# Two more groups of the second down block by seven products, their sums of weights formed in HBM by adding transfers

## The chip, the cores and the metric

The kernel runs on one core of a Trainium2 chip. The metric is the device time of one execution in microseconds, a median over several runs. Engines are named as in the profile: PE (TensorE matmuls), PEld (its weight loads), DVE (VectorE), ACT (ScalarE), POOL (GpSimd), SP (SyncE, which here only issues transfers). Transfers run on 16 DMA engines, which the queues of SP, ACT and POOL share.

## What is computed

One layer on 256 tokens of width 2048, in float32: three kinds of attention, a gated merge, an output product, and a feed-forward part. The change is in the last product, `w_down`:

```python
h2 = rms_norm(x, g_ffn[l])
u = causal_depthwise_conv(h2 @ w_up[l], conv_w[l], conv_b[l])
u_gate, u_val = jnp.split(u, 2, axis=-1)
x = x + (jax.nn.silu(u_gate) * u_val) @ w_down[l]      # [256, 5632] @ [5632, 2048]
```

## The kernel before

**Precision.** Every weight tile is split into two float32r tiles, `hi` (a cast on ACT) and `lo = raw - hi` (a subtract on DVE). The activations are split in the same way. A product is three matmuls: `hi*hi`, `lo*hi`, `hi*lo` (`three`). Weights come from HBM through a ring of raw tiles (six of 128x1024 in the last stages), and `hi` and `lo` have four buffers each.

**The order of the stages.** The products of `mem` (`kv`, at the very start, one k of 128 rows at a time: 512 KB of `w_mem_kv`, and pieces of `mem`, then of `x`, which PE transposes), the projections with the attention heads between them, the gates, the branches and the merge, the output product, the up product with its convolution (from about 778 to 1232 us, a `tick` of the background work at every pair of k), and the down product in two blocks of 1024 columns (block 0 from about 1232 us, block 1 from 1344 us).

**Groups by eight or by seven.** A group of the down product is two k-tiles of 128 rows (`a_pair(p)`) by 1024 columns, and 256 tokens: a 2x2 by 2x2 block product with blocks of 128x128 and 128x512. `eight` does the eight block products, from two raw tiles. `seven` does seven, from sums of blocks of weights (T1, T2, T3, T4) and sums of blocks of activations (FS1 to FS4). The activation sums are made by `form` (and `pair_sums`), up to eight short operations on DVE and some casts on ACT. The weight sums are made ahead of time: `pair_sums_ahead` loads 1 MB of weights into SBUF, adds on DVE (`sums_in`), and stores the four sums to HBM in a tile `kept` (columns T1, T3, T4, T2 of `[P, 4, 512]`), mostly as background work in the up stage. `seven` then reads two of the blocks of `w_down` and the four sums: one whole raw tile (B10, B11), one of B00 and T3, one of T1 and T2, and half a tile of T4 (`junk`, two buffers).

**The plans.** A string says for each of a block's 22 groups whether it goes by eight (`e`) or by seven (`s`); `f` is a call of `form`, which readies the sums of the next pair. The sums of pairs 11 and later are kept where activations of pairs already used by an `e` lay (`s_of`). Block 0 has 11 sevens and 11 eights; block 1 has 14 and 8.

**What sets the order.** A scheduler places instructions on each engine as early as their inputs allow, unless they are pinned (`in_order`, `pin`). SP's queue takes loads in the order in which they were placed; each load waits until its raw tile is free, that is for the `lo` subtract of the tile six loads before. POOL has some masks to make at the start, transfers of small rows at 182 to 189 us and at 759 to 769 us, masks of attention heads between, and nothing else.

Of the kernel before, what the change touches and what calls it, by code (L numbers as in the profile page):

```python
# [13 lines left out]
ALU = mybir.AluOpType  # L14
# [19 lines left out]
PIECE = 1024  # L34
# [9 lines left out]
def hybrid_block(  # L44
# [25 lines left out]
    nc = tc.nc  # L70
# [31 lines left out]
    background = []  # L102
# [101 lines left out]
    def k_tiles(name):  # L204
# [23 lines left out]
    g_plans = (("", "esesesee", "esesesee"), ("esesesee", "esesesee", "esesesee"))  # L228
    d_plans = (
        "efefefef" + "sef" * 4 + "ssefsfssfssee",  # L230
        "efefef" + "sss" + "esss" * 3 + "ssee",
    )
    T1, T3, T4, T2 = range(4)
    FS2, FS4, FS3, FS1 = range(4)
    in_order = tc.keep_in_program_order
    dram = ctx.enter_context(tc.tile_pool(name="dram", bufs=1, space=bass.MemoryType.DRAM))
    by_k = lambda w: w[0].rearrange("(k p) n -> p k n", p=P)
# [6 lines left out]
        for name, w, plans in (("o", w_out, o_plans), ("d", w_down, d_plans))  # L244
        for nb, plan in enumerate(plans)
        for pr in pairs(name, plan.count("s"))
        for h in range(2)
    )

    def sums_in(w):  # L250
        both = w[:, 1:2].to_broadcast([P, 2, w.shape[2]])
        in_order(nc.vector.tensor_tensor(w[:, 0:2], w[:, 0:4:3], both, ALU.add))
        in_order(nc.vector.tensor_tensor(w[:, T2], w[:, T1], w[:, T2], ALU.add))
        in_order(nc.vector.tensor_tensor(w[:, T4], w[:, T2], w[:, T4], ALU.add))

    def kept_for(name, nb, pr):
        if (name, nb, pr) not in sums_of:
            at = f"kept_{name}{nb}_{pr}"
            sums_of[name, nb, pr] = dram.tile([P, 4, 512], F32, tag=at, name=at)
        return sums_of[name, nb, pr]  # L260
# [24 lines left out]
    def pair_sums_ahead(staging, period, add, store, most=99, delay=0):  # L285

        due = deque()
        clock = 0
        for _ in range(delay):
            yield  # L290

        def step():
            while due and due[0][0] <= clock:
                _, kept, w = due.popleft()
                in_order(nc.sync.dma_start(kept, w))

        periods = cycle(period if isinstance(period, tuple) else (period,))
        while len(halves) > 1 and halves[0][-1] == 0 and most:
            most -= 1
            name, wv, nb, pr, _ = halves.popleft()  # L300
            halves.popleft()
            kept = kept_for(name, nb, pr)
            w = staging(f"pre_{name}{nb}_{pr}")
            in_order(
                nc.sync.dma_start(
                    w.rearrange("p (k c) -> p k c", k=2), wv[:, 2 * pr : 2 * pr + 2, nb * PIECE : (nb + 1) * PIECE]
                )
            )
            w = w.rearrange("p (i c) -> p i c", i=4)
            due.append((clock + store, kept, w))  # L310
            for t in range(next(periods)):
                if t == add:
                    sums_in(w)
                step()
                clock += 1
                yield
        while due:
            step()
            clock += 1
            yield  # L320

    def first_sums():

        name, wv, nb, pr, _ = halves.popleft()
        halves.popleft()
        kept = kept_for(name, nb, pr)
        two = []
        for h in range(2):
            w = block(f"pre_{name}{nb}_{pr}_{h}").rearrange("p (i c) -> p i c", i=4)
            two.append(w)  # L330
            n0 = nb * PIECE + h * 256
            for n in range(2):
                in_order(
                    nc.sync.dma_start(
                        w.rearrange("p (k n) c -> p k n c", k=2)[:, :, n],
                        wv[:, 2 * pr : 2 * pr + 2, n0 + n * 512 : n0 + n * 512 + 256],
                    )
                )
            yield
            yield  # L340
        for w in two:
            sums_in(w)
            yield
        for _ in range(3):
            yield
        for h, w in enumerate(two):
            in_order(nc.sync.dma_start(kept[:, :, h * 256 : (h + 1) * 256], w))
            yield
# [475 lines left out]
    def in_turn(name):  # L824
        turn[0] += 1
        return staged[:, turn[0] % 2]

    background.append(pair_sums_ahead(in_turn, PF, 3, 7, most=14))
    qm = heads_of(block("qm"))
    y = norm_heads(ps, rstd, "mq")  # L830
# [348 lines left out]
    for nb, plan in enumerate(o_plans):  # L1179
# [19 lines left out]
    ends_tile = lambda name, dt: ff.tile([P, 2, PIECE], dt, tag="ends", bufs=1, name=name)  # L1199
    background.append(  # L1200
        pair_sums_ahead(lambda name: ends_tile(name, F32).rearrange("p i c -> p (i c)"), 8, 1, 5, delay=DU)
    )

    def a_pair(p):
        if p < FA // 2:
            return aT[:, 2 * p : 2 * p + 2]
        if not ends:
            ends.append(ends_tile("a_ends", F32R).rearrange("p i (k c) -> p i k c", k=2))
        return ends[0][:, p - FA // 2]
# [64 lines left out]
    for f0 in range(0, FT, 4):  # L1274
# [5 lines left out]
        for s in range(2):  # L1280
            ps = [bank(f"u{f0 + i}_{s}") for i in range(4)]
            c0 = s * D_FF + f0 * P
            for k in range(0, KT, 2):
                hi, lo = piece(upv[:, k : k + 2, c0 : c0 + 512], 2, 512, f"u{f0}_{s}_{k}")
                for j in range(2):
                    first, last = k + j == 0, k + j == KT - 1
                    for i in range(4):
                        c = slice(i * P, (i + 1) * P)
# [23 lines left out]
    N0, N1 = (plan.count("s") for plan in d_plans)  # L1312
# [3 lines left out]
    a_blocks = aT.rearrange("p k (l t q) -> p k l t q", l=2, t=NT)  # L1316
    formed = [0]

    def s_of(p, f):


        if f == FS1:
            return a_blocks[:, 2 * p, :, 1]
        if p < 9:
            return sf[:, 3 * p + f]
        if p == 9:
            return sf_more[0][:, f] if f < 2 else sf_rest[2]
        if p == 10:
            return sf[:, 27] if f == 0 else sf_rest[f - 1]
        return a_blocks[:, 2 * (p - N0 + N1) + f // 2, :, f % 2]  # L1330

    tmp_d = lambda name: place([P, PIECE], F32, "ts", name)

    def form():
        p = formed[0]
        formed[0] += 1
        if p == 9:
            sf_rest.extend(cst.tile([P, 2, P], F32R, tag=tag, name=f"sf_{tag}") for tag in ("rbc", "taps", "rows"))
        if p < 9:
            groups = [(sf[:, 3 * p : 3 * p + 3], slice(0, 3))]  # L1340
        elif p == 9:
            sf_more.append(place([P, 2, 2, P], F32R, "sf", "sf_more"))
            groups = [(sf_more[0], slice(0, 2)), (sf_rest[2], 2)]
        else:
            groups = [(s_of(p, f), f) for f in range(3)]
        pair_sums(a_pair(p), tmp_d(f"fw_{p}"), groups + [(s_of(p, FS1), FS1)])
# [4 lines left out]
    for nb, plan in enumerate(d_plans):  # L1351
        apart = [] if nb == 1 else None
        X = blocked(
            "d", w_down, nb, nb * PIECE, plan, lambda p, j: a_pair(p)[:, j], s_of, raw_d, junk,
            lambda n0, Y: gather(n0, Y, tmp_d), None, form, apart,
        )
        for t in range(NT):
            for n in range(2):
                c = nb * PIECE + n * 512
                o = xres[:, t, c : c + 512]  # L1360
                nc.vector.tensor_tensor(o, o, X[t][n], ALU.add)
                if (nb, t, n) == (1, 1, 1):
                    nc.scalar.dma_start(ov[:, t, c : c + 256], o[:, :256])
                    c, o = c + 256, o[:, 256:]
                    nc.vector.tensor_tensor(o, o, apart[0], ALU.add)
                    nc.scalar.dma_start(ov[:, t, c : c + 256], o)
                else:
                    nc.scalar.dma_start(ov[:, t, c : c + 512], o)
# [31 lines left out]
```

## Time and profile before

| | us |
|---|---|
| median of 3 runs | 1460.6 (1460.43, 1460.6, 1470.62) |
| the profiled execution | 1459.85 |
| its span, first to last instruction | 1458.1 |
| PE busy, by the records | 1452.6 |
| DVE busy | 1222.1 |
| ACT busy | 852.3 |
| DMA, mean of the span | 266 GB/s |

Times in the profile are counted from the start of the span. Busy time of PE counts matmuls whose ends are modelled and which overlap, so the distance from one matmul's start to the next says more than the length of one. A wait is idle time of an engine put down to what ended it.

### The profile page before, as it was taken

To read this page: it belongs to the slowest core of one execution; us is meant where nothing else is said; L and a number is where in the kernel's file an instruction comes from. 1 tells how busy PE (TensorE), PEld (TensorE's weight loads), DVE (VectorE), ACT (ScalarE), POOL (GpSimd) and SP (SyncE) were. 2 spreads that over 40 slices of the span, in tenths; PEclk is the share of its full clock that TensorE was granted. 3 is DMA by queue.
4 is the path that set the end of the run, shared out by engine and by line. 5 is a ranking of instruction groups with operands and counts; after the bars stand their busy time and mean duration, and the time that the engine had idled before them with its cause. 6 is when DMAs were issued, how large, how long until landed. Compare 5 with 4: busy or idle time off the path is not lost.

```text
span 1458.1 us, 20568 instructions
## 1 busy us (share of the span) xinstructions
PE 1452.6 (100%) x7295; PEld 1228.6 (84%) x7295; DVE 1222.1 (84%) x1804; ACT 852.3 (58%) x1210; POOL 21.4 (1%) x52
## 2 busy tenths in 40 slices
PE   9999999999999999999999999999999999999998
PEld 7888888888888888888888888888888888888887
DVE  5788778776898899998987888888888877999878
ACT  6755445464564556546766656556556565676665
POOL 0000010010000000000000000000000000000000
PEclk9999999999999999999999999999999999999999
DMA  8797999777668576788877888888888866789896
GB/s 294 227 351 246 324 330 329 261 256 218 205 210 267 174 227 200 269 269 263 300 214 233 290 273 299 283 269 300 287 278 299 271 197 201 255 282 339 297 333 218
DMA packets 166502, 387.64 MB, mean 266 GB/s; under 512 B 12554, under 2 KB 29854, under 8 KB 162174
## 3 DMA queue, kind: packets, MB, share of 16 engines
q1 hardware_dynamic: 164702, 383.29, 79.7%
q10 hardware_dynamic: 1328, 2.11, 0.4%
q8 instruction: 57, 0.93, 0.3%
q0 software_dynamic: 368, 0.93, 0.2%
q14 instruction: 47, 0.39, 0.1%
HBM read 347.47 MB, written 38.80 MB: 265 GB/s over the span
## 4 chain that ended last, share of the span: by engine, by line
PE 94%; DVE 3%; issue 2%; DMA 1%; POOL 0%; ACT 0%; DVEq 0%; POOLq 0%; ACTq 0%
PE u L1289 22%; PE u L1290 11%; PE xd L362 4%; PE xd L360 4%; PE xd L361 3%; PE xg L362 3%; PE xg L360 3%; PE xg L361 3%; PE s L362 2%; PE f L362 2%; PE s L360 2%; PE f L360 2%; PE f L361 2%; PE b L362 2%; PE s L361 2%; PE b L360 2%
## 5 line engine op out<-in xcount | busy, mean ns | idle before, releaser
L1289 PE MATMUL u<-hT,hi_u 128*128 128x512 f32 x1232 | 428.3, 394 | 0.0
L1290 PE MATMUL u<-hT,lo_u 128*128 128x256 f32 x1232 | 341.3, 277 | 0.0
L144 DVE TENSOR_TENSOR lo_u<-raw_u,hi_u 128x1024 fp32r<-128x1024 f32 x176 | 215.0, 1222 | 73.3 <-ACT hi_u L143 72.5
L1289 PEld LDWEIGHTS u<-hT,hi_u 128*128 128x128 f32 x1232 | 231.0, 188 | 53.6
L143 ACT CAST hi_u<-raw_u 128x1024 fp32r<-128x1024 f32 x176 | 184.7, 1050 | 133.8 <-PE u L1289 99.4
L1290 PEld LDWEIGHTS u<-hT,lo_u 128*128 128x128 f32 x1232 | 231.3, 188 | 0.0
L355 DVE TENSOR_TENSOR lo_d<-raw_d,hi_d 128x1024 fp32r<-128x1024 f32 x88 | 106.8, 1222 | 16.5 <-ACT hi_d L354 14.1
L354 ACT CAST hi_d<-raw_d 128x1024 fp32r<-128x1024 f32 x88 | 91.8, 1054 | 39.3 <-PE xd L361 13.1
L354 ACT CAST hi_g<-raw_g 128x1024 fp32r<-128x1024 f32 (+1 forms) x80 | 77.1, 972 | 49.4 <-PE xg L361 19.4
L355 DVE TENSOR_TENSOR lo_g<-raw_g,hi_g 128x1024 fp32r<-128x1024 f32 (+1 forms) x80 | 88.6, 1119 | 4.1 <-ACT hi_g L354 4.1
L361 PE MATMUL xg<-hi_g,xT 128*128 128x512 f32 x175 | 68.1, 389 | 0.0
L362 PE MATMUL xg<-lo_g,xT 128*128 128x512 f32 x175 | 68.1, 389 | 0.0
L360 PE MATMUL xg<-hi_g,xT 128*128 128x512 f32 x175 | 68.1, 389 | 0.0
L143 ACT CAST hi_f<-raw_f 128x1024 fp32r<-128x1024 f32 (+1 forms) x40 | 38.5, 967 | 46.3 <-PE f L361 29.4
L144 DVE TENSOR_TENSOR lo_s<-raw_s,hi_s 128x1024 fp32r<-128x1024 f32 (+1 forms) x40 | 44.5, 1119 | 23.8 <-ACT hi_s L143 23.8
L1289 PE MATMUL u<-hT_rest,hi_u 128*128 128x512 f32 x176 | 62.0, 394 | 0.0
L143 ACT CAST hi_b<-raw_b 128x1024 fp32r<-128x1024 f32 x32 | 33.7, 1053 | 45.9 <-PE b L361 20.3
L143 ACT CAST hi_s<-raw_s 128x1024 fp32r<-128x1024 f32 (+1 forms) x40 | 38.4, 962 | 37.7 <-PE s L361 26.8
L1240 ACT ACTIVATE y<-u,taps 128x256 f32<-128x256 f32 x88 | 49.6, 596 | 16.8 <-DVE u L1235 16.7
L144 DVE TENSOR_TENSOR lo_f<-raw_f,hi_f 128x1024 fp32r<-128x1024 f32 (+1 forms) x40 | 44.4, 1116 | 17.4 <-ACT hi_f L143 17.2
L362 PE MATMUL xd<-lo_d,aT 128*128 128x512 f32 x148 | 57.6, 389 | 0.0
L360 PE MATMUL xd<-hi_d,aT 128*128 128x512 f32 x148 | 57.6, 389 | 0.0
(551 smaller groups left out, 3482.0 us busy)
## 6 DMA issues: line engine op xcount, KB each, us to landing
raw_u<-in_w_up_dram SPq DMA_DIRECT2D x176, 512.0 KB, 4.8
raw_g<-in_w_in_dram SPq DMA_DIRECT2D x96, 512.0 KB, 4.5
raw_d<-in_w_down_dram SPq DMA_DIRECT2D x63, 512.0 KB, 5.5
pre_d<-in_w_down_dram SPq DMA_DIRECT2D x17, 1024.0 KB, 7.4
kept_d<-pre_d SPq DMA_DIRECT2D x17, 1024.0 KB, 7.0
raw_f<-in_w_in_dram SPq DMA_DIRECT2D x32, 512.0 KB, 5.6
raw_s<-in_w_in_dram SPq DMA_DIRECT2D x32, 512.0 KB, 6.1
raw_t_d<-kept_d SPq DMA_DIRECT2D x25, 512.0 KB, 5.8
```

The lines of the kernel that those rows point to most:

```text
L143: pin(nc.scalar.copy(hi[:, :m], raw[:, :m]))
L144: pin(nc.vector.tensor_tensor(lo[:, :m], raw[:, :m], hi[:, :m].bitcast(F32), ALU.subtract))
L354: nc.scalar.copy(hi[:, :n], src)
L355: nc.vector.tensor_tensor(lo[:, :n], src, hi[:, :n].bitcast(F32), ALU.subtract)
L360: fix(nc.tensor.matmul(o, lhsT=ah, rhs=w[0], start=first, stop=False))
L361: fix(nc.tensor.matmul(o, lhsT=al, rhs=w[0], start=False, stop=False))
L362: fix(nc.tensor.matmul(o, lhsT=ah, rhs=w[1], start=False, stop=last))
L1240: nc.scalar.activation(y, u[:, 2:], AF.Identity, scale=tap(2), bias=tap(3))
L1289: nc.tensor.matmul(ps[i], lhsT=hi[:, j, c], rhs=hT(k + j), start=first, stop=False)
L1290: nc.tensor.matmul(ps[i][:, :S], lhsT=lo[:, j, c], rhs=hT(k + j)[:, :S], start=False, stop=last)
```

## The change

Block 1 of the down product gets 16 sevens and 6 eights. The plan has two more `s` and `f` and is laid out anew; the activation sums of pairs 11 to 15 lie three to a pair, densely, behind the 32 k-tiles that belong to sevens (`s_of`). The weight sums of pairs 14 and 15 of this block (`in_hbm`) don't go through SBUF and DVE: a new generator, `sums_in_hbm`, issues five transfers for each on POOL's queue. The first copies the four blocks of weights from `w_down` into `kept`, the next four add one block onto another in place: T1 = B00 + B01, T3 = B01 + B11, T2 = T1 + B11, T4 = T2 + B10.

```diff
     d_plans = (
         "efefefef" + "sef" * 4 + "ssefsfssfssee",
-        "efefef" + "sss" + "esss" * 3 + "ssee",
+        "efsss" * 3 + "efssfsssssee",
     )
+    in_hbm = (("d", 1, 14), ("d", 1, 15))
...
         for pr in pairs(name, plan.count("s"))
+        if (name, nb, pr) not in in_hbm
         for h in range(2)
...
+    def sums_in_hbm(delay, period):
+        for _ in range(delay):
+            yield
+        for name, nb, pr in in_hbm:
+            kept = kept_for(name, nb, pr)
+            wv = by_k(w_down)[:, 2 * pr : 2 * pr + 2, nb * PIECE : (nb + 1) * PIECE]
+            b = wv.rearrange("p k (n c) -> p k n c", n=2)
+            nc.gpsimd.dma_start(kept.rearrange("p (k n) c -> p k n c", k=2), b)
+            for _ in range(period):
+                yield
+            for dst, src in ((0, b[:, 0, 1]), (1, b[:, 1, 1]), (3, kept[:, 0]), (2, kept[:, 3])):
+                nc.gpsimd.dma_start(kept[:, dst], src, accum_op=ALU.add)
+                for _ in range(period):
+                    yield
...
+    background.append(sums_in_hbm(40, 8))
...
-        return a_blocks[:, 2 * (p - N0 + N1) + f // 2, :, f % 2]
+        i = 3 * (p - N0) + f
+        return a_blocks[:, 2 * N1 + i // 2, :, i % 2]
```

The generator waits for 40 ticks of the up stage before its first transfer, but these transfers aren't pinned. POOL's order, before, from its last masks at the start of the kernel to the first mask of an attention head (`kept_d_14` and `kept_d_15` are the sums of pairs 14 and 15, `ck_row` and `ck` the small rows at 182 to 189 us):

```order
L557 AFFINE_SELECT upto<-ones_r 128x128
L561 AFFINE_SELECT after_r<-ones_r 128x128
L897 DMA ck_row_1832<-logits 128x2x4
L897 DMA ck_row_1836<-logits 128x2x2
L899 DMA ck_1834<-ck_row_1832 128x1024
L899 DMA ck_1838<-ck_row_1836 128x512
L926 AFFINE_SELECT fx_1959<-fx_1959 128x128 x2
```

And the same place now:

```order
L578 AFFINE_SELECT after_r<-ones_r 128x128
L331 DMA kept_d_14_7922<-in_w_down_dram 256x1x1024
L331 DMA kept_d_15_9059<-in_w_down_dram 256x1x1024
L335 DMA kept_d_14_7922<-in_w_down_dram 128x512 x2
L335 DMA kept_d_15_9059<-in_w_down_dram 128x512 x2
L335 DMA kept_d_14_7922<-kept_d_14_7922 128x512
L335 DMA kept_d_15_9059<-kept_d_15_9059 128x512
L335 DMA kept_d_14_7922<-kept_d_14_7922 128x512
L335 DMA kept_d_15_9059<-kept_d_15_9059 128x512
L914 DMA ck_row_1832<-logits 128x2x4
```

All ten transfers stand at the start of POOL's program, ahead of everything that POOL does for the attention; the only waits among them are those of each add for the transfers of its own pair.

DVE at the seam of the two down blocks, before (`xres_again` is the residual, to which block 0's last bank `xd_1_1` is added; `fw` and `aT` are the steps of `form`; `lo_d_30` is the split of k-tile 30, `lo_t_d_0` that of the sums of pair 0):

```order
L1361 TENSOR_TENSOR xres_again<-xres_again,xd_1_1_11735 128x512
L369 TENSOR_TENSOR fw_12858<-aT 128x512
L355 TENSOR_TENSOR lo_d_30_12874<-raw_d_30_12871,hi_d_30_12873 128x1024
L372 TENSOR_TENSOR fw_12858<-fw_12858 128x256
L373 SCALAR_TENSOR_TENSOR fw_12858<-fw_12858 128x128
L355 TENSOR_TENSOR lo_d_31_12892<-raw_d_31_12889,hi_d_31_12891 128x1024
L374 TENSOR_TENSOR fw_12858<-fw_12858 128x128
L378 TENSOR_TENSOR aT<-fw_12858,aT 128x128 x4
L355 TENSOR_TENSOR lo_d_32_12923<-raw_d_32_12920,hi_d_32_12922 128x1024
L369 TENSOR_TENSOR fw_12907<-aT 128x512
L355 TENSOR_TENSOR lo_d_33_12941<-raw_d_33_12938,hi_d_33_12940 128x1024
```

And now:

```order
L1380 TENSOR_TENSOR xres_again<-xres_again,xd_1_1_11746 128x512
L386 TENSOR_TENSOR fw_12870<-aT 128x512
L372 TENSOR_TENSOR lo_d_0_12897<-raw_d_0_12887,hi_d_0_12896 128x1024
L389 TENSOR_TENSOR fw_12870<-fw_12870 128x256
L390 SCALAR_TENSOR_TENSOR fw_12870<-fw_12870 128x128
L372 TENSOR_TENSOR lo_d_1_12907<-raw_d_1_12890,hi_d_1_12906 128x1024
L391 TENSOR_TENSOR fw_12870<-fw_12870 128x128
L395 TENSOR_TENSOR aT<-fw_12870,aT 128x128 x4
L372 TENSOR_TENSOR lo_t_d_0_12917<-raw_t_d_0_12892,hi_t_d_0_12916 128x1024
L372 TENSOR_TENSOR lo_t_d_0_12927<-raw_t_d_0_12894,hi_t_d_0_12926 128x512
L386 TENSOR_TENSOR fw_13061<-aT 128x512
L372 TENSOR_TENSOR lo_d_2_12943<-raw_d_2_12933,hi_d_2_12942 128x1024
```

The first seven of block 1 (pair 0) follows its first eight (pair 16) at once, where two more eights stood between; the second `form` stands behind the splits of that seven.

## The prediction

> **What bounds the kernel now.** I read the page first: busy times, then the slices.
>
> ```profile
> PE 1452.6 (100%) x7295; PEld 1228.6 (84%) x7295; DVE 1222.1 (84%) x1804; ACT 852.3 (58%) x1210; POOL 21.4 (1%) x52
> PE   9999999999999999999999999999999999999998
> PEclk9999999999999999999999999999999999999999
> DMA  8797999777668576788877888888888866789896
> ```
>
> TensorE is busy in every slice at its full clock, while the DMA engines are 60 to 90% busy. Matmul ends are modelled, so I went next to the waits of PE over the whole span; these two rows are all there are.
>
> ```profile
> PE spare L93 <- DVE qscale L565: 1.2, 1, 1.2
> PE s L362 <- DVE lo_s L144: 0.2, 1, 0.2
> ```
>
> Nothing holds PE up after the first 1.2 us. The span is its matmuls laid end to end; the timeline gives their pitch, here at the start of down block 1 (rows 3 matmuls apart).
>
> ```profile
> 1343.81 0.39 PE L360 MATMUL xd<-hi_d,aT 128*128 128x512 f32 x1
> ...
> 1344.49 0.39 PE L360 MATMUL xd<-hi_d,aT 128*128 128x512 f32 x1
> ...
> 1345.85 0.39 PE L360 MATMUL xd<-hi_d,aT 128*128 128x512 f32 x1
> ```
>
> Nine matmuls take 2.04 us: 0.227 us each, not the 0.39 of one record. So two things decide: how many matmuls go, and whether any supply of PE becomes late. A microsecond lost anywhere is lost for good, since PE has no later wait to make it up in.
>
> **Part 1, the products.** `eight` calls `three` 8 times (24 matmuls), `seven` 7 times (21). Two groups change from one to the other: 6 x 0.227 = 1.4 us less on PE. This lies on the path: **-1.4**.
>
> **Part 2, the supply of down block 1.** A seven needs 3.5 splits of 1024 columns where an eight needs 2, so DVE gets 2 x 1.5 = 3 more subtracts; and `form` runs 5 times there, not 3.
>
> ```profile
> L355 DVE TENSOR_TENSOR lo_d<-raw_d,hi_d x45: 1214/1224/1226, 1334.9 to 1445.4; 128x1024 fp32r<-128x1024 f32 x45
> L369 DVE TENSOR_TENSOR fw<-aT x3: 682/684/693, 1344.8 to 1355.3; 128x512 f32<-128x512 f32 x3
> L372 DVE TENSOR_TENSOR fw<-fw x3: 415/415/417, 1346.5 to 1357.1; 128x256 f32<-128x256 f32 x3
> L378 DVE TENSOR_TENSOR aT<-fw,aT x12: 280/284/286, 1348.5 to 1360.3; 128x128 fp32r<-128x128 f32 x12
> 1340.00:1350.00 10.00, 10.00 (x46) 8.29 (x45) 9.93 (x18) 4.78 (x8) 0.00 (x0) 1.00 0.96 319
> 1350.00:1360.00 10.00, 10.00 (x46) 8.29 (x45) 9.34 (x19) 5.19 (x12) 0.00 (x0) 1.00 0.89 305
> 1420.00:1430.00 10.00, 10.00 (x46) 8.25 (x45) 8.11 (x8) 7.37 (x8) 0.00 (x0) 1.00 0.92 328
> ```
>
> (In the window rows: length, then PE, PEld, DVE, ACT and POOL busy, granted clock, DMA share, GB/s.) Three subtracts are 3.7 us; a form is 0.68 + 0.42 + two 128-column steps at about 0.28 + 4 x 0.28 = 2.8, two are 5.6. DVE gets 9.3 us more over some 100 us. It is 99 and 93% busy only where three forms and the rest of block 0 come together, and 81% later. The change puts one form into that crowded stretch in place of three and the rest further on. Going through the DVE rows of the two orders with these durations, the first split of each of the first three sevens is ready 1 to 1.7 us before PE reaches it, about as in the steady sevens before. I cost it at nothing; without that cover each form would show with up to 2.8 us.
>
> The transfers are tighter. A seven reads seven pieces of 128x512 of 4 bytes, 1792 KB, in 21 x 0.227 = 4.77 us, which is 385 GB/s; an eight 1024 KB in 5.45 us, 193 GB/s.
>
> ```profile
> 1410.00:1420.00 10.00, 10.00 (x46) 8.29 (x45) 7.51 (x8) 5.90 (x6) 0.00 (x0) 1.00 0.99 342
> 1430.00:1440.00 10.00, 10.00 (x46) 8.29 (x45) 8.70 (x9) 7.80 (x10) 0.00 (x0) 1.00 1.00 344
> 1413.45 1.05 ACT L354 CAST hi_d<-raw_d 128x1024 fp32r<-128x1024 f32 x1 [0.61 <-DMA raw_d<-kept_d]
> 1438.00 1.57 ACT L354 CAST hi_t_d<-raw_t_d 128x1024 fp32r<-128x1024 f32 x2 [0.65 <-DMA raw_t_d<-kept_d]
> ```
>
> At a share of 1.00 the engines move 344 GB/s, so in an unbroken run each seven falls 1835/344 - 4.77 = 0.56 us behind. The longest run is 5 now and becomes 7. After 5 the cast waits 0.65 us and PE not at all, because the four `hi` and `lo` buffers stand between; two more sevens add 1.1 us of lateness, about what those buffers hold. I take **0**, with 0 to 2 us kept for the range.
>
> **Part 3, the ten transfers of the sums.** The generator says tick 40 of the up stage, but the order of POOL shows them right behind its last start-up instruction, waiting only for one another. In the trace that instruction stands here, and POOL then has nothing to do until 182 us.
>
> ```profile
> 1.85 0.28 POOL L561 TENSOR_SCALAR_AFFINE_SELECT after_r<-ones_r 128x128 fp32r<-128x128 f32 x1
> ```
>
> So the copies start at about 2.2 us. What they meet, by windows of the start:
>
> ```profile
> 2.50:5.00 2.50, 2.50 (x9) 1.04 (x7) 0.65 (x2) 0.62 (x1) 0.00 (x0) 1.00 0.88 274
> 5.00:7.50 2.50, 2.47 (x7) 1.86 (x7) 1.69 (x4) 0.62 (x1) 0.00 (x0) 1.00 0.87 254
> 7.50:10.00 2.50, 2.50 (x12) 1.79 (x11) 1.55 (x3) 1.50 (x3) 0.00 (x0) 1.00 1.01 356
> 10.00:12.50 2.50, 2.50 (x14) 2.08 (x13) 1.83 (x4) 2.02 (x4) 0.00 (x0) 1.00 1.06 409
> 15.00:20.00 5.00, 5.00 (x26) 4.11 (x25) 3.05 (x6) 3.58 (x8) 0.00 (x0) 1.00 1.02 295
> 30.00:40.00 10.00, 10.00 (x51) 7.99 (x49) 7.66 (x18) 7.35 (x17) 0.00 (x0) 1.00 0.75 239
> ```
>
> Here DMA is full from 7.5 us on and nearly full before. And this is where PE has no reserve, by the rows of the weights of the fourth k (SP's issue, cast, subtract, first matmul on it):
>
> ```profile
> 5.68 0.80 SPq L142 DMA_DIRECT2D raw_kv<-in_w_mem_kv_dram  x1
> 12.77 1.05 ACT L143 CAST hi_kv<-raw_kv 128x1024 fp32r<-128x1024 f32 x1 [0.57 <-DMA raw_kv<-in_w_mem_kv_dram]
> 13.85 1.23 DVE L144 TENSOR_TENSOR lo_kv<-raw_kv,hi_kv 128x1024 fp32r<-128x1024 f32 x1 [0.75 <-ACT hi_kv L143]
> 15.86 0.39 PE L154 MATMUL kv<-hi_kv,memT 128*128 128x512 f32 x1
> ```
>
> The cast waits for the transfer until 12.77; the split is done at 15.08, and PE needs it at 15.86: 0.8 us in hand. By then SP has had to bring 2 MB of weights and 1 MB of `mem`. The two copies are 2 x 1 MiB = 2.1 MB. Some 0.2 MB of it finds room from 2.5 to 7.5 us, where an eighth is free; the other 1.9 MB pushes the loads back, at the 383 GB/s that the two full windows have on average by 5.0 us. Of this 0.8 is covered: PE waits 4.2 us, in pieces from about 9 us on.
>
> Then the eight adds, 256 KB each. No row shows an adding transfer, nor one from HBM to HBM. The nearest rows are a plain store and POOL's own transfers:
>
> ```profile
> kept_d<-pre_d SPq DMA_DIRECT2D x17, 1024.0 KB, 7.0
> ck<-ck_row POOLq DMA_DIRECT2D x1, 512.0 KB, 9.0
> ```
>
> From below they are plain copies: 2.1 MB, 6 us of the engines, spread in three dependent rounds over 20 us or more, beside loads that need 239 of some 344 GB/s: hidden, 0. From above they take the engines four times as long, 24 us (first rival below). I take twice a copy, since an add also reads where it writes: 12 us of the engines from 15 to 45 us, of which the 25% that are free in the 30 to 40 us window hide 7; the loads' own reserve (four weight tiles, refilled as PE runs) takes 3. That leaves **+2**. With the copies: **+6.2**, between 0 and about 19.
>
> [...] No run here shows two full queues together.
>
> **The sum.** The profiled execution took 1459.85 us (span 1458.1 and 1.75 around it), 0.75 under the median of 1460.6. 1459.85 - 1.4 + 0 + 6.2 = **1464.6**.
>
> **Rivals.**
> - *The adds are dear (slower).* If an adding transfer holds the engines four times as long as a copy, 2.1 MB takes 24 us of them; sharing evenly with the loads it lasts from 15 to about 65 us, and loads that need 70% of the engines get 50% for these 50 us: 29% of 50 = 14.5 us lost, 4.2 before that: 1459.85 - 1.4 + 18.7 = 1477. It ends past one per cent from about four times a copy's price on. For it: nothing is known of the price, and DMA is at 0.75 and above for most of the first 40 us. Against it: the rounds wait for each other, so the engines get pauses.
> - *All is hidden (not slower).* If the copies are served slowly, or behind SP's, PE never waits: 1459.85 - 1.4 = 1458.5. For it: in the first 5 us the share is still below 0.9, and POOL's 512 KB took 9 us to land beside SP's loads, so its queue is no fast one. Against it: the 0.8 us in hand at the fourth k.
> - *PE slows down after the wait.* The first matmuls of the kernel ran at half the later rate:
>
> ```profile
> 1.23 2.42 PE L93 MATMUL spare<-idle 128*128 128x384 bf16 x7 [1.23 <-DVE qscale L565]
> ```
>
>   2.42/7 is 0.35 us for 384 columns, 0.9 ns each, against 0.227/512 = 0.44 ns later. If a wait of 4.2 us in one piece brings that state back, and it takes as long again to leave, half of 4.2 is lost: +2.1, 1466.7. [...] The page's clock row shows 1.00 throughout, so it doesn't show the state even where the pitch does.
>
> **How the numbers follow.** The forecast, PE waits of 2 to 9 us in the first 50 us (1460.5 to 1467.5): 0.43. All hidden, 1458.3 to 1460.5: 0.26. The slower state on top, about 1467: 0.11. Adds between twice and four times a copy, 1467.5 to 1475: 0.10. Dearer still, over 1475.2: 0.09. Something that makes it over 1% faster: 0.01; no mechanism gives it, as only 1.4 us of matmuls go. One per cent is 14.6 us, about what a measurement of this kernel can tell from no change. Within it: 0.43 + 0.26 + 0.11 + 0.10 = 0.90. The range goes from 1458.3 (all hidden) to 1472, which leaves out 0.09, some 0.04 of the case before it and 0.01. It takes in the 0 to 2 us of the run of sevens.
>
> **What would show it.** Right: rows of POOL issuing ten transfers from about 2 us; a cast of `hi_kv` that waits several us for `raw_kv` around 10 to 17 us; new rows of PE or PEld waiting on `lo_kv` or `hi_kv`, together some 6 us; every later stage the same length and shifted; down block 1 shorter by 1.4. Wrong: no wait at the start; or waits of PE in the last run of sevens, on `lo_t_d`; or transfers of the sums that are still under way at 60 us; or sums that begin in the up stage.

## The result and the profile after

| | before | after |
|---|---|---|
| median, us | 1460.59 | 1473.09 |
| lowest to highest, us | 1459.89 to 1470.62 | 1470.53 to 1480.56 (8 runs) |
| ratio, 95% interval | | 1.0083 (1.0065 to 1.0100) |
| the profiled execution, us | 1459.85 | 1474.6 |
| its span, us | 1458.1 | 1472.9 |

The changed kernel is 12.5 us slower. The forecast was 4 us and its range ended at 1472.0, 1.1 us below the median. In several of the kernels here, the one before among them, single executions take some 9 us more than the others (1469.29 and 1470.62 of the eight before, 1480.56 of the eight after), and the medians leave these out.

The page first, in the same rows as before: busy times, then PE, its granted clock and the DMA engines in 40 slices of 37 us.

```profile
PE 1458.9 (99%) x7289; PEld 1230.3 (84%) x7289; DVE 1229.3 (83%) x1824; ACT 857.1 (58%) x1222; POOL 29.5 (2%) x62
PE   7999999999999999999999999999999999999998
PEclk8999999999999999999999999999999999999999
DMA  9888799868667667697877888888888866789996
```

There are six matmuls fewer, as the change says. Only the first slice is different: PE is idle there, and its clock is below full. The waits of PE, which were two rows before, say for what (line, what it waited for, us in total, times, longest).

```profile
PE mT L197 <- DMA memres<-in_mem_dram: 3.9, 3, 2.8
PE kv L154 <- ACT memT L183: 1.4, 1, 1.4
PE kv L156 <- DVE lo_kv L144: 1.2, 3, 0.5
PE kv L154 <- ACT hi_kv L143: 1.2, 3, 0.7
...
PE kv L155 <- DVE memT L186: 0.4, 1, 0.4
```

All five are of the first stage (the rest is 1.2 us at the very start, as before, and 0.5 us in a projection): the pieces of `mem` (`memres`, then `memT` behind PE's transpose), and the casts and splits of `w_mem_kv`, which themselves wait for their transfers. The rows add up to 8.1 us, about half of what this execution loses at the start (15.9 us, below). Each counts only from the modelled end of the matmul before it, and some twenty matmuls at half clock, 0.43 us apart and not 0.227, took about 4 us more. POOL's rows show what was in the way.

```profile
2.10 1.50 POOL L331 DMA_DIRECT2D kept_d<-in_w_down_dram  x2
11.32 1.77 POOL L335 DMA_DIRECT2D kept_d<-in_w_down_dram  x2 [7.73 <-DMA kept_d<-in_w_down_dram]
...
35.39 0.81 POOL L335 DMA_DIRECT2D kept_d<-kept_d  x1 [2.47 <-DMA kept_d<-kept_d]
```

The copies are issued at 2.1 us and the last add at 35.4 us. How much of the DMA engines they took is read from the queues between 0 and 50 us (packets, MB, share of the 16 engines over these 50 us), before:

```profile
q1 hardware_dynamic: 8486, 13.82, 85.3%
```

and after:

```profile
q1 hardware_dynamic: 6237, 9.62, 58.7%
q0 software_dynamic: 1696, 4.19, 38.4%
```

q1 is SP's queue of loads, q0 is POOL's. Together they fill 97% of these 50 us; the loads got 26.6% of 50 us = 13.3 us less of the engines than before and brought 4.2 MB less. The same place of the program stands later by about as much: POOL's small rows for the attention, before and after.

```profile
182.72 1.59 POOL L897 DMA_DIRECT2D ck_row<-logits  x2 [180.58 <-DVE logits L894]
```

```profile
198.63 1.50 POOL L914 DMA_DIRECT2D ck_row<-logits  x2 [162.44 <-DVE logits L911]
```

They come 15.9 us later. The span is only 14.8 longer, so everything behind that place became 1.1 us shorter. Down block 1, with its last runs of sevens, is in these windows of after (length; PE, PEld, DVE, ACT, POOL busy; clock, DMA share, GB/s).

```profile
1420.00:1430.00 10.00, 10.00 (x46) 8.29 (x45) 7.14 (x10) 6.38 (x10) 0.00 (x0) 1.00 0.99 359
1440.00:1450.00 10.00, 10.00 (x45) 8.28 (x45) 9.00 (x10) 7.81 (x9) 0.00 (x0) 1.00 1.05 410
```

The DMA engines are full there and PE has no gap.

### The profile page after: what moved, and what is told of

Its sections match the earlier page's. It is cut to its first block, busy times and chain, and to the rows that moved or that the text cites. A ratio compares the mean times of both kernels' runs of the same rounds, so it can differ in the third digit from the quotient of the medians.

```text
span 1472.9 us, 20626 instructions
## 1 busy us (share of the span) xinstructions
PE 1458.9 (99%) x7289; PEld 1230.3 (84%) x7289; DVE 1229.3 (83%) x1824; ACT 857.1 (58%) x1222; POOL 29.5 (2%) x62
## 4 chain that ended last, share of the span: by engine, by line
PE 93%; DMA 3%; DVE 2%; issue 1%; SPq 0%; POOL 0%; ACT 0%; DVEq 0%; POOLq 0%; ACTq 0%
PE u L1307 22%; PE u L1308 11%; PE xd L379 3%; PE xd L378 3%; PE xd L377 3%; PE xg L379 3%; PE xg L378 3%; PE xg L377 3%; PE s L379 2%; PE s L377 2%; PE f L377 2%; PE f L379 2%; PE f L378 2%; PE b L379 2%; PE s L378 2%; PE b L377 2%
## 5 line engine op out<-in xcount | busy, mean ns | idle before, releaser
L372 DVE TENSOR_TENSOR lo_d<-raw_d,hi_d 128x1024 fp32r<-128x1024 f32 x88 | 106.8, 1223 | 13.4 <-ACT hi_d L371 11.5
L371 ACT CAST hi_t_g<-t_g 128x1024 fp32r<-128x1024 f32 x30 | 31.5, 1051 | 39.7 <-PE xg L378 34.7
L371 ACT CAST hi_t_d<-raw_t_d 128x1024 fp32r<-128x1024 f32 (+1 forms) x54 | 43.5, 835 | 18.6 <-PE xd L378 10.6
```

The source lines that it names most:

```text
L371: nc.scalar.copy(hi[:, :n], src)
L372: nc.vector.tensor_tensor(lo[:, :n], src, hi[:, :n].bitcast(F32), ALU.subtract)
```

## The experiments

Eleven kernels ran, on three chips. The kernel before took 1460.34 us on the chip of start_only, spaced, copies_only and plain, 1461.27 on that of at_k8, pinned, warm and copies_1k, and 1461.15 on that of plain_twice, gates and spaced_again.

**start_only: is it the start alone?** The kernel before, its plans untouched, with the ten transfers added as they are in the changed kernel; nothing reads the sums.

```diff
+    in_hbm = (("d", 1, 14), ("d", 1, 15))
...
+    background.append(sums_in_hbm(40, 8))
```

> The plans of before; the ten transfers of the sums are issued as in the changed kernel, and nobody reads their sums. Theory (all of the loss lies in the first 50 us): PE's products are those of before, so it should take about 1.4 us more than the changed kernel, 1472 to 1476, and the first cast of the k-tiles after the squares should come 14 to 17 us later than before. Rival (the new plan of down block 1 starves PE): it should take about what before took, 1460 to 1463.

1472.66 us, ratio 1.0076 (1.0048 to 1.0104): 12.3 us over the kernel before, inside the range expected. The start of the changed kernel costs 13.9 us (12.5, and 1.4 that the products save), 1.6 more, which lies within the intervals of the two ratios. So the loss comes without the new plan of block 1. What stands behind the first stage comes 12.7 us later (the first cast of `hi_mq`, at 64.31 against 51.63 us), where 14 to 17 was expected. The windows of its first stage will be needed for the clock below.

```profile
10.00:20.00 10.00, 6.81 (x28) 4.33 (x29) 3.62 (x6) 3.22 (x6) 4.07 (x5) 1.00 1.06 296
20.00:30.00 10.00, 6.88 (x22) 4.33 (x21) 2.31 (x4) 3.16 (x6) 0.81 (x1) 0.83 1.02 256
```

**spaced and spaced_again: the change without the start.** Each transfer is pinned to its tick in the up stage and waits for the PE instruction placed last before it.

```diff
+    def after_pe(ins):
+        in_order(ins)
+        last = next(i for i in reversed(nc.cur_bb.bb.instructions) if i.engine == mybir.EngineType.PE)
+        tc.add_manual_dep(
+            ins.ins, last.name, mybir.DependencyInfo(mybir.DependencyClass.Sync, mybir.DependencyReason.DATA), reason="paced"
+        )
...
-            nc.gpsimd.dma_start(kept.rearrange("p (k n) c -> p k n c", k=2), b)
+            after_pe(nc.gpsimd.dma_start(kept.rearrange("p (k n) c -> p k n c", k=2), b))
...
-                nc.gpsimd.dma_start(kept[:, dst], src, accum_op=ALU.add)
+                after_pe(nc.gpsimd.dma_start(kept[:, dst], src, accum_op=ALU.add))
```

> The changed kernel with its ten transfers pinned to the up stage, each waiting for the matmul that stood last when it was traced, from tick 40 on, 8 ticks apart. Theory (only the start is lost): the start is that of before and the two groups save their 1.4 us, so 1458.5 to 1460, with no wait of PE in the up stage, where the four weight tiles ahead cover a transfer that comes alone. Rival (down block 1 loses by itself): 1462 or more, with waits of PE after 1340 us. Rival (an adding transfer disturbs the loads wherever it runs): 1462 or more, with waits of PE between 980 and 1200 us.

> The changed kernel with its ten transfers in the up stage, 22 us apart, a second time, to narrow the ratio. Theory that the products' 1.4 us are a gain once the transfers are hidden: 1.0 to 1.5 us below the kernel before, 0.9990 to 0.9993. Rival that the transfers or the run of sevens give it back: 1.000.

The first time 1459.31 us, ratio 0.9994 (0.9971 to 1.0018); the second time 1459.18 us, ratio 0.9980 (0.9965 to 0.9995), which leaves out 1. By medians it is 1.0 and 2.0 us faster than the kernel before; the 1.4 us of the products lies between (the second was expected at 1.0 to 1.5). The second run's rows of POOL, of its queue from 850 to 1080 us, and all waits of PE in the whole span:

```profile
857.33 0.68 POOL L338 DMA_DIRECT2D kept_d<-in_w_down_dram  x1 [88.50 <-PE u L1315]
879.53 0.91 POOL L342 DMA_DIRECT2D kept_d<-in_w_down_dram  x1 [21.52 <-PE u L1315]
...
1057.01 0.81 POOL L342 DMA_DIRECT2D kept_d<-kept_d  x1 [21.37 <-PE u L1315]
```

```profile
q0 software_dynamic: 1696, 4.19, 8.2%
```

```profile
PE spare L93 <- DVE qscale L589: 1.2, 1, 1.2
PE s L386 <- DVE lo_s L144: 0.3, 1, 0.3
PE xg L386 <- DVE lo_t_g L379: 0.2, 1, 0.2
```

The same ten transfers take 8.2% of 230 us, 18.9 us of the engines, about what they take at the start, and PE waits for nothing new. It is faster than both kernels, so the sevens, the `form`s and the denser `s_of` cost block 1 nothing that shows.

**copies_only: the copies' share.** The loop of adds is left out.

```diff
-            for dst, src in ((0, b[:, 0, 1]), (1, b[:, 1, 1]), (3, kept[:, 0]), (2, kept[:, 3])):
-                nc.gpsimd.dma_start(kept[:, dst], src, accum_op=ALU.add)
-                for _ in range(period):
-                    yield
```

> The eight adds are left out, so the sums of two groups are wrong; the two copies stay at the start. By the working of the prediction the copies alone make PE wait 4.2 us: about 1463. If most of the loss is the copies (they starve the first loads, and PE then runs at half its clock): 1467 to 1470. If the adds are the dear part: 1460 to 1465.

1463.94 us, ratio 1.0019 (1.0006 to 1.0032): 4.7 us over the spaced kernel (1459.2). PE has one long wait in the first stage, and three of 0.4 us.

```profile
PE mT L197 <- DMA memres<-in_mem_dram: 3.3, 1, 3.3
```

PE's transposes of the next two pieces of `mem`, before and here:

```profile
7.50 0.38 PE L197 MATMUL mT<-ident,memres 128*128 128x128 f32 x2
...
10.72 0.60 PE L197 MATMUL mT<-ident,memres 128*128 128x128 f32 x4
```

```profile
10.46 0.44 PE L197 MATMUL mT<-ident,memres 128*128 128x128 f32 x2 [3.28 <-DMA memres<-in_mem_dram]
...
15.51 0.60 PE L197 MATMUL mT<-ident,memres 128*128 128x128 f32 x4
```

The first stand 3.0 us later, the second 4.8. Between them PE waits 0.43 us; the other 1.4 are matmuls at 0.43 us each, where 0.23 were due. How the two queues shared the engines shows in this run's window from 7.5 to 10 us (POOL's queue, then SP's):

```profile
q0 software_dynamic: 194, 0.74, 72.2%
q1 hardware_dynamic: 190, 0.29, 30.8%
```

They moved about as many packets each, but POOL's were 3.8 KB on the mean and SP's 1.5, so POOL had 72% of the engines.

**plain and plain_twice: is it the adding, or the time of the engines?** In plain, each add becomes a plain copy of the same 256 KB. In plain_twice, each becomes two, the second into a tile that nobody reads.

```diff
-                nc.gpsimd.dma_start(kept[:, dst], src, accum_op=ALU.add)
+                nc.gpsimd.dma_start(kept[:, dst], src)
+                nc.gpsimd.dma_start(spare[:, dst], src)
```

> The eight adds are plain copies of the same blocks in the same order with the same waits, so the sums of two groups are wrong. Theory (an add costs the engines more than a copy, since it reads where it writes): 3 to 7 us less than the changed kernel, 1466 to 1470. Rival (it is the count and place of the transfers, not the adding): within 1.5 us of the changed kernel.

> The changed kernel with each of the eight adds at the start replaced by two plain copies of the same 256 KB, one to the place of the add and one to a tile that nobody reads (the sums of weights of two groups are left out). Theory that an add costs PE what its 12 us of the 16 DMA engines cost, whatever they do in that time, because nothing in the first stage is left to hide them: the 16 copies take about the same 12 us, and the kernel takes 1472 to 1475 us, as the changed kernel. Rival that the adding itself delays the loads (a read and a write of the same place, more packets, one transfer waiting for another) beyond the time it takes from the engines: 16 plain copies are served beside the loads like eight, and it stays at 1466 to 1469.

plain: 1466.16 us, ratio 1.0028 (1.0012 to 1.0044). plain_twice: 1477.24 us, ratio 1.0097 (1.0072 to 1.0122), 2 us above what was expected and far from the rival's 1466 to 1469. POOL's queue from 0 to 50 us in copies_only, plain and plain_twice, in this order:

```profile
q0 software_dynamic: 544, 2.10, 11.6%
```

```profile
q0 software_dynamic: 1184, 4.19, 24.0%
```

```profile
q0 software_dynamic: 1824, 6.29, 44.1%
```

With the row of the changed kernel (38.4%) this is the price of engine time in the first stage. The last column is the median less the 1459.2 us of the spaced kernel, which has the same matmuls.

| at the start | us of all 16 engines | median, us | PE pays, us |
|---|---|---|---|
| two copies | 5.8 | 1463.94 | 4.7 |
| and eight plain copies | 12.0 | 1466.16 | 7.0 |
| and eight adds (the change) | 19.2 | 1473.09 | 13.9 |
| and sixteen plain copies | 22.1 | 1477.24 | 18.0 |

The eight adds take 19.2 - 5.8 = 13.4 us of the engines, eight plain copies 6.2: an add costs 2.2 times a copy. The price of a copy isn't fixed, though: the sixteen of plain_twice took 16.3 us and not 12.4, and by these an add costs 1.6 times. This also fits the 2 us by which plain_twice went past its expected range. Sixteen plain copies cost PE more than eight adds, so the loss needs no delay by the adding as such. From the second row on, a microsecond of the engines costs PE about one: 10.1 us more from plain to plain_twice cost 11.1 (10.3, if the 0.8 us between the times of before on the two chips is taken off). The first 6.2 us behind the copies cost only 2.2, so about 4 us are hidden, and no more. POOL's packets behind the copies rise in the same order (640, 1152 and 1280), so these runs don't tell engine time from the number of packets.

**copies_1k: smaller rows.** As copies_only, with each copy cut into four in rows of 1 KB.

```diff
-            nc.gpsimd.dma_start(kept.rearrange("p (k n) c -> p k n c", k=2), b)
+            for k, h in ((0, 0), (0, 1), (1, 0), (1, 1)):
+                c = slice(h * 256, (h + 1) * 256)
+                nc.gpsimd.dma_start(kept[:, 2 * k : 2 * k + 2, c], b[:, k, :, c])
```

> Only the copies, as in the run without adds, so the sums of two groups are wrong; but in rows of 1 KB where they had 4 KB. If the engines take packets in turn from each queue (so that large rows push out the small rows of mem): the first wait for memres is shorter than 3.3 us, and the time is 1460 to 1463. If only the sum of the bytes counts: the same as with rows of 4 KB, 1463 to 1465, or more, since small rows cost more.

1465.86 us, ratio 1.0032 (1.0021 to 1.0042), 4.6 over the kernel before on its chip, against 3.6 for copies_only. PE waits for `memres` twice, 2.9 and 1.1 us, where it waited 3.3 once, and then 1.7 us for `memT`.

```profile
PE mT L197 <- DMA memres<-in_mem_dram: 4.0, 2, 2.9
```

But the packets didn't become smaller with the rows. POOL's queue from 0 to 50 us:

```profile
q0 software_dynamic: 640, 2.10, 12.3%
```

Each transfer shows 16 packets of 4 bytes beside its data. Without them 512 packets are left of these 640 and 512 of the 544 of copies_only, 4 KB each in both. So the run doesn't settle what shorter packets would do. It shows that the same packets from eight transfers, issued over 5.6 us and not 1.5, cost no less. PE's clock stayed at 1.00 all the time, and the loss was no smaller for it. That smaller packets cost more shows elsewhere, in SP's queue in the trace of the kernel before: one of 4 KB took 159 ns by the median and one of 1 KB 46 ns, 16% more for the same bytes (4% by the means, 191 and 49.6 ns).

**warm: is it the halved clock?** PE's clock falls to half between 20 and 30 us of the changed kernel, in this window and in the timeline of PE.

```profile
20.00:30.00 10.00, 8.55 (x22) 5.46 (x21) 2.01 (x3) 1.85 (x4) 1.62 (x2) 0.50 0.99 214
```

```profile
23.44 0.63 PE L155 MATMUL kv<-hi_kv,memT 128*128 128x512 f32 x1
23.87 0.63 PE L156 MATMUL kv<-lo_kv,memT 128*128 128x512 f32 x1
24.30 0.63 PE L154 MATMUL kv<-hi_kv,memT 128*128 128x512 f32 x1
```

The pitch is 0.43 us against 0.227. warm puts matmuls on unused data ahead of the places where PE waits.

```diff
+            keep_busy(12)
             to_mT(1, 1)
...
+        if 0 < k < 9:
+            keep_busy(6)
```

> The changed kernel with matmuls on an idle tile put into the gaps of the first stage (12 before the second transposes, 6 before each of the next eight k), about 1 us each time, so that PE doesn't fall to half its clock. If the halved clock is a large part of the loss (theory: 4 to 6 us of the 14): 1467 to 1470. If PE only waits for loads and the clock hides in those waits: 1472 to 1476, since a slow matmul that ends before the next load lands costs nothing.

1478.75 us, ratio 1.0120 (1.0105 to 1.0135), 5.7 more than the changed kernel: a miss for both. The added matmuls lie in PE's queue and are paid for, and the clock was still 0.83 from 20 to 30 us. It doesn't settle what the clock cost. start_only says more: with a clock of 0.83 in the one window, and 1.00 in the one before it, it lost 12.3 us where the changed kernel lost 13.9 with 0.50.

**at_k8, pinned and gates: the transfers in one burst elsewhere.** The ten transfers follow one another, only later: at the ninth k of the first product (36 us), at the start of the up stage (770 us), and at the gates of the second half (489 us).

```diff
             xT = k_tiles("xT")
+            deque(sums_in_hbm(0, 0), 0)
```

```diff
     for m in range(2):
+        if m == 1:
+            deque(sums_in_hbm(0, 0), 0)
```

The first diff is that of at_k8, the second that of gates; both use `after_pe` for the transfers. pinned has `in_order` there, and no wait for PE.

> The changed kernel with the ten transfers still back to back, but held until the matmuls of the eighth k of the first stage (about 34 us before), when four weight tiles are ahead and the DMA share is 0.75. Theory (the transfers hurt because PE has no reserve in the first 15 us): the same transfers cost 0 to 3 us here, 1459 to 1462, and the clock stays at 1.00. Rival (18 us of the engines are lost wherever the transfers lie close together): 1466 or more.

> The ten transfers pinned behind POOL's last rows, so back to back from about 770 us, where the up stage begins and its loads have four tiles in hand. Theory: 1459 to 1461, as in the paced kernel. Rival (close together they stall any stage): 1463 or more, with waits of PE on lo_u or hi_u.

> The changed kernel with its ten transfers back to back, held until PE begins the gates of the second half (about 490 us), where the DMA share before was 0.28 from 490 to 500 us, 0.61 and 0.72 in the next two windows. Theory that the price is engine time that finds no room: 18 us of engines find 7 + 4 + 3 us free in these 30 us, so nearly all is hidden: 1458.5 to 1461. Rival that a burst on POOL's queue delays a load there whatever the share is, as it did when held until 36 us (1464.9) or 770 us (1468): 1463 to 1470.

The theory missed in all three; pinned and gates came out where their rivals had them, at_k8 between the two. at_k8: 1464.89 us, ratio 1.0023 (1.0013 to 1.0033), 5.6 over spaced; the clock stayed at 1.00, and PE's new waits are in the projections and heads that follow. pinned: 1468.24 us, ratio 1.0040 (1.0023 to 1.0057), with single runs from 1458.66 to 1472.12. gates: 1466.76 us, ratio 1.0037 (1.0017 to 1.0057), 7.6 over spaced, although the windows of the kernel before seemed to have room there:

```profile
490.00:500.00 10.00, 10.00 (x50) 8.38 (x49) 7.60 (x10) 6.51 (x8) 0.00 (x0) 1.00 0.28 73
500.00:510.00 10.00, 10.00 (x45) 8.27 (x45) 8.47 (x10) 5.59 (x7) 0.00 (x0) 1.00 0.61 200
```

The timeline of gates shows how a burst costs PE more than the wait itself (DVE's row of a weight sum, then PE).

```profile
510.62 0.69 DVE L496 TENSOR_TENSOR t_g<-raw_g 128x512 f32<-128x512 f32 x1 [5.48 <-DMA raw_g<-in_w_in_dram]
```

```profile
508.80 0.39 PE L385 MATMUL xg<-hi_t_g,xT 128*128 128x512 f32 x1
512.51 0.80 PE L386 MATMUL xg<-lo_t_g,xT 128*128 128x512 f32 x1 [3.32 <-DVE lo_t_g L379]
513.10 0.63 PE L384 MATMUL yg<-hi_t_g,xs 128*128 128x512 f32 x1
...
518.22 0.46 PE L384 MATMUL xg<-hi_g,xT 128*128 128x512 f32 x1
518.52 0.40 PE L385 MATMUL xg<-hi_g,xT 128*128 128x512 f32 x1
```

DVE waits 5.48 us for one load. PE should have gone on at 509.03 and goes on at 512.51: 3.5 us. The 13 matmuls from there to 518.22 take 5.71 us, where 13 x 0.227 = 2.95 were due: 2.8 more. With one wait of 0.8 us later, on `lo_g`, these are 7.1 of the 7.6 us. The average share of 10 us hides how the loads come, in clumps: in windows of 2 us the share before is 0.00 at 496 us and 0.98 four microseconds later.

```profile
496.00:498.00 2.00, 2.00 (x10) 1.66 (x9) 2.00 (x3) 1.70 (x3) 0.00 (x0) 1.00 0.00 0
...
500.00:502.00 2.00, 2.00 (x10) 1.65 (x10) 2.00 (x4) 0.29 (x2) 0.00 (x0) 1.00 0.98 365
```

The profiled execution of pinned took 1462.06 us, one of its shorter ones, with one long wait:

```profile
PE u L1308 <- DVE lo_u L144: 1.9, 1, 1.9
```

What makes its median 6 us longer than that was not seen and stays open.

## Why the prediction was wrong

**The place and the mechanism were right.** The ten transfers are issued from 2.1 us, push back the loads of the first stage, make PE wait there and hardly anywhere else (0.5 us in a projection), and the later stages are only shifted. start_only loses about as much without the new plan.

**The products: right.** Predicted -1.4; what lies behind 200 us is 1.1 shorter, and spaced is 1.0 and 2.0 us faster than the kernel before.

**The supply of block 1: right at 0.** No wait of PE in the longer runs of sevens, with the engines at a share of 0.99 and 1.05.

**The copies: the size right, partly by luck; the place wrong.** Predicted 4.2 us, measured 4.7. The prediction read PE's reserve from the weights of the fourth k, 0.8 us, and expected its waits from about 9 us on, on `lo_kv` or `hi_kv`. In copies_only PE stops at 7.2 us already, at the second k, and for a piece of `mem`, 3.3 us at once; slow matmuls behind it, 0.43 us apart, bring most of the rest (1.4 us).

**The adds: the step that failed.** The prediction put them at twice a copy, "12 us of the engines from 15 to 45 us, of which the 25% that are free in the 30 to 40 us window hide 7; the loads' own reserve (four weight tiles, refilled as PE runs) takes 3. That leaves +2". The 12 us were well sized (13.4 in the changed kernel); that an add reads where it writes, the reason given for "twice", no run shows by itself. The hiding was not: 13.4 us of engines cost PE 1473.09 - 1463.94 = 9.2 us, so 4 us were hidden and not 10. Two things were wrong in it. The 25% belong to 30 to 40 us alone, but were taken over all 30 us from 15 to 45, of which the half up to 30 us had shares of 1.02 (15 to 20 us) and 1.00 (20 to 30). And the free time was counted for a schedule that no longer held: the loads that the copies had pushed back by 4 us come due in it. In the changed kernel the window is full:

```profile
30.00:40.00 10.00, 9.09 (x42) 6.36 (x40) 4.02 (x6) 5.74 (x12) 1.63 (x2) 0.99 1.04 291
```

A balance over the whole stretch would have come out better: the transfers take 19.2 us, the queues before left under 15% of 50 us = 7 free, so about 12 us of loads come late, where the forecast had 6.2 and the measured price is 13.9. The prediction did have a case for 1467.5 to 1475, at a chance of 0.10, but for adds dearer than it took them; the adds were about as dear as it took them, and less of them was hidden.

**The rivals.** "All is hidden" fell at the start, and is what spaced reaches. "The adds are dear" named the right effect, late loads for some 40 us, but at four times a copy's price, and it is 2.2. "PE slows down after the wait" was partly so. The prediction said that the clock row doesn't show this state; it does, at 0.50. At the start no run shows that it costs more than the loads do: copies_1k lost no less than copies_only with its clock at 1.00, since PE then waited longer; whether the 1.6 us between start_only and the changed kernel are the clock's is not shown. In gates PE ran on without a wait until 544 us, so there it costs 2.8 us on top of a wait of 3.5. The prediction's 2.1 us took the slow state to last as long as the wait, which was its author's estimate. In gates the slow matmuls are 0.427 us apart (3.84 us for nine from 514.38 us on), and 5.7 us after the wait of 3.5 the distance falls to 0.30 and then 0.23 us. start_only shows the half clock behind shorter waits too: its matmuls are 0.43 us apart from 24.12 us on, behind waits of 1.2 and 0.5 us, and no wait of PE before them was over 1.3 us.

The forecast's 4.2 and 6.2 us take it that POOL's transfers are served beside SP's loads at once, and "The adds are dear" that the two share the engines evenly; both were the author's assumptions, and no run ahead of the change shows either. What the runs showed in their place is copies_only from 7.5 to 10 us: 194 packets of POOL's queue went beside 190 of SP's, and had 72% of the engines. That this is why a piece of `mem` was the first to be late is argued, not shown.

## What to carry to other kernels

Before an extra transfer is called hidden, add up the engine time of everything that must land between two points of the schedule, the pushed-back loads too; a free share read from the trace of before can be spent once, and only in the windows that show it. Where PE has a few microseconds of loads in hand, spread the transfers so that each one fits into that reserve: in spaced some 19 us of engines cost nothing that shows when each transfer was held 22 us from the next, and 6 to 14 us when they came in one burst (at_k8, gates, the start), even at a place with a mean share of 0.28 to 0.72. A transfer that nothing pins goes to where its inputs allow, here the start of the program, so its delay has to be a dependence.

## What the runs showed that was not expected

- An adding transfer from HBM to HBM took the DMA engines 2.2 times as long as a plain copy of the same 256 KB (13.4 against 6.2 us for eight; 1.6 times against the sixteen copies of plain_twice). It goes in packets of 2 KB, the plain copy in packets of 4 KB, though the rows are 2 KB in both: without the 16 small ones an add has 128 packets and a copy 64 (1696 and 1184 for all ten transfers). By these sums a packet took 0.21 us of its engine in an add and 0.19 in a copy, so a byte of an add cost twice as much.
- In copies_only, from 7.5 to 10 us, the queues of POOL and SP moved about as many packets each, 194 of 3.8 KB on the mean and 190 of 1.5 KB.
- One wait of 3.3 us was followed by 5.7 us at half clock (gates), so it cost 6.2.
- With the burst at 770 us (pinned) eight of ten runs took 1467.25 to 1472.12 us, the others 1458.66 and 1462.06. With the same transfers held apart, 20 of 22 runs lie between 1457.95 and 1461.24. What made the eight long was not seen.
